# Two FFN layers around a mixer: where the norms' transposes stand, and how far the second token half trails

## The chip, the cores and the metric

The kernel runs on one core of a Trainium2 chip. The metric is device microseconds of one execution, as the median of several runs. Shorter is better.

## What is computed

One decoder layer over 256 tokens of width 2048, in float32. `layer_norm` has scale and shift. The middle line stands for a mixer of differential attention and an RWKV-7 scan with one input projection of 6432 columns; only its output projection matters here.

```python
x = layer_norm(alpha * x + 0.5 * swiglu(x, ffn1_w_gate, ffn1_w_up, ffn1_w_down), ln1_g, ln1_b)
mix = concat([diff_attention(x @ w_in), rwkv7(x @ w_in)]) @ w_out
x = layer_norm(alpha * x + mix, ln2_g, ln2_b)
x = layer_norm(alpha * x + 0.5 * swiglu(x, ffn2_w_gate, ffn2_w_up, ffn2_w_down), ln3_g, ln3_b)

def swiglu(x, w_gate, w_up, w_down):
    return (silu(x @ w_gate) * (x @ w_up)) @ w_down
```

## The kernel before, in words

**Weights and tokens.** The 256 tokens are two halves of 128. Weights come from memory in *pairs*: two blocks of 128 rows by 512 columns, 512 KB, into one of three `raw` buffers (L121, on SyncE's queue). ScalarE rounds a pair to a high part `wh` (L131), VectorE takes the difference as a low part `wl` (L132), and one pair costs each token half six matmuls in `product`: high by high (L139), high by low (L140), low by high (L141). `wh` and `wl` stand in numbered slots, seven in the FFNs and five in the mixer (`NW`). A slot is written anew only when both halves' matmuls with its old pair are done. A `raw` buffer is free when its L132 is done, and only then does the next load into it start.

**Lag.** `block` runs a pair for the first half at once and keeps the second half's turn in a list `pend`, which holds up to `lag` pairs: four in the FFNs, two in the mixer (`LAG`). The first half's sum so ends some pairs before the second half's.

**The FFN's block product.** `two_blocks` does two column blocks for both halves. Of the first eight row blocks it makes seven products in place of eight, of sums and differences of weights and of tokens. Six accumulator banks of PSUM have roles, `a, z, u, w, v, s` in `self.roles`, which change places from one call to the next. The remaining row blocks are done as ordinary pairs (`later`, `late`). At the end of an FFN six such pairs are left for the last block; `flush(lag)` runs them with the second half `lag` pairs behind (L459). At that time the first half's sum is in the bank of role `u` and the second half's in that of `v`.

**The norm.** When a half's last sum is there, `down_done` adds it to the residual (L449; in the mixer `o_done`, L1064), takes statistics (L450 or L1066), and `ln_tail` does the rest on VectorE: L305, L307, a power on GpSimd (L309, 1.0 us), then for each of four column blocks the scaling in two steps (L313, L314). For the norms 1 and 2 each block is then transposed on TensorE in four matmuls by the identity (L76), and split on ScalarE (`xh`, L82) and VectorE (`xl`, L83) as the left operand of the next stage. For norm 3 the blocks go to the output.

**Banks of the transposes.** `tr_bank` gives a bank for each transpose. In the FFNs `ffn_bank` takes, for two of three norm blocks, a bank that it counts from `stream.rot` and from its own count, and a bank `tr` for the third. `rot` isn't changed by `two_blocks`, so which role stands in the bank that is taken isn't looked at.

**The output projection.** The rows of `w_out` come in three parts: the first attention half and the first scan half, then the second attention half, then the second scan half (L1066 belongs to the third part). The third part needs the end of the scan: L863, L869, the head norm (L884, L885, L888, L894 to L899), L902, L904, the gate (L915, L918, L919) and the split of its result (L82, L83). It has four column blocks of two pairs.

**Order.** The program is written in one order, and a scheduler puts each engine's instructions in a row after its own estimate of their times. Each engine then runs its row strictly as it stands.

Of the kernel before, what the change touches and what calls it, by code (L numbers as in the profile page):

```python
# [30 lines left out]
LAG = {"ffn": 4, "mix": 2}  # L31
NW = {"ffn": 7, "mix": 5}
# [7 lines left out]
def build(tc, A, out):  # L40
# [15 lines left out]
    def nm(s):  # L56
        uid[0] += 1
        return f"{s}_{uid[0]}"
# [241 lines left out]
    stream = Stream()  # L300
# [20 lines left out]
    def load_gb(pool, g, b, tg, tb):  # L321
        gt = hp.tile([P, D], F32, tag=tg, name=nm("lng"))
        bt = pool.tile([P, D], F32, tag=tb, name=nm("lnb"))
        nc.gpsimd.dma_start(out=gt, in_=g.to_broadcast([P, D]))
        nc.gpsimd.dma_start(out=bt, in_=b.to_broadcast([P, D]))
        return [[t[:, q * NB:(q + 1) * NB] for q in range(4)] for t in (gt, bt)]

    def load_gb_over_x(g, b):
        gb = [[], []]
        for q in range(4):  # L330
            for i, (t, a) in enumerate((("xh", g), ("xl", b))):
                o = xp.tile([P, NB], F32, tag=f"{t}1{q}", name=nm("lngb"))
                nc.gpsimd.dma_start(out=o, in_=a[:, q * NB:(q + 1) * NB].to_broadcast([P, NB]))
                gb[i].append(o)
        return gb

    def ffn(fp, wg, wu, wd, lg, lb, res, last, extra=None):
# [47 lines left out]
        for half, nj in enumerate((6, 5)):  # L385
# [70 lines left out]
                stream.two_blocks(((wd, n * NB), (wd, (n + 1) * NB)), ks, h_lhs, comb, lambda i, tt, acc, n=n, f=down_done: f(tt, acc, n + i))  # L456
            if half == 1:
                gb.extend(load_gb_over_x(lg, lb))
                stream.flush(LAG["ffn"])  # L459
            j0 += nj  # L460


# [52 lines left out]
    def mix(mp, pq, C):  # L515
# [521 lines left out]
        def ready(q):  # L1037
            stream.drain(gens((a1, a2, r1, r2)[q]))
            for tt in range(2):
                split(res[q][:, :, tt * P:(tt + 1) * P], oT, tt, q)  # L1040
# [16 lines left out]
        def o_done(tt, acc, n, i):  # L1057
            c = slice(n * NB, (n + 1) * NB)
            if i == 0:
                rc = mp.tile([P, NB], F32, tag="tm", name=nm("rc"), bufs=2)  # L1060
                nc.scalar.dma_start(out=rc, in_=xs[tt][:, c])
                V.scalar_tensor_tensor(out=y[tt][n], in0=rc, scalar=ALPHA, in1=acc, op0=ALU.mult, op1=ALU.add)
            else:
                V.tensor_tensor(out=y[tt][n], in0=y[tt][n], in1=acc, op=ALU.add)  # L1064
            if i == len(parts) - 1:
                V.bn_stats(out=st[tt][:, n, :], in_=y[tt][n])  # L1066
                if n == 3:
                    ln_tail(tt, y[tt], st[tt], gb[0], gb[1], False)

        for i, qs in enumerate(parts):  # L1070
            for q in qs:
                ready(q)
            if i == 0:
                yt = [hp.tile([P, 4, NB], F32, tag="J0", name=nm("y")), mp.tile([P, 4, NB], F32, tag="BKc", name=nm("y"))]
                y = [[yt[n // 2][:, 2 * (n % 2) + t, :] for n in range(4)] for t in range(2)]
            if 3 in qs:
                gb.extend(load_gb(mp, A["ln2_g"], A["ln2_b"], "J1", "Q"))
            ks = [(4 * q + j, 4 * q + j) for q in qs for j in range(4)]
            for n in range(4):
                stream.block(A["w_out"][0], n * NB, NB, ks, o_lhs, lambda tt, acc, n=n, i=i: o_done(tt, acc, n, i))  # L1080


    def ffn_bank(pool):
        n = [0]

        def bank(spare=False):
            n[0] += 1
            if spare and n[0] % 3:
                i = (stream.rot + n[0] % 3) % NACC["ffn"]
                return (pa if i < 3 else pool).tile([P, 4, P], F32, tag=f"acc{i}", name=nm("tr"))  # L1090
            return pool.tile([P, 4, P], F32, tag="tr", name=nm("tr"), bufs=2)

        return bank

    with tc.tile_pool(name="fp1", bufs=1) as fp, tc.tile_pool(name="pt1", bufs=1, space=bass.MemoryType.PSUM) as pt:
        tr_bank.append(ffn_bank(pt))
        stream.phase("ffn", fp, pt)
        xc = [fp.tile([P, D], F32, tag=f"y{tt}", name=nm("xc")) for tt in range(2)]

        def load_x(tt, q):  # L1100
            c = slice(q * NB, (q + 1) * NB)
            nc.sync.dma_start(out=xc[tt][:, c], in_=A["x"][0, tt * P:(tt + 1) * P, c])
            transpose_split(xc[tt][:, c], tt, q, xT, tt == 0 and q < 2)

        for q in range(4):
            stream.hooks[2 * q] = [lambda q=q, t=t: load_x(t, q) for t in range(2)]
        xr = [A["x"][0, t * P:(t + 1) * P, :] for t in range(2)]
        C = {}
        ffn(fp, A["ffn1_w_gate"][0], A["ffn1_w_up"][0], A["ffn1_w_down"][0], A["ln1_g"], A["ln1_b"], xr, False,
            lambda after: C.update(mixer_consts(fp, after)))  # L1110
        stream.flush()
    with tc.tile_pool(name="mp", bufs=1) as mp, tc.tile_pool(name="pq", bufs=1, space=bass.MemoryType.PSUM) as pq:
        stream.phase("mix", mp)
        mix(mp, pq, C)
        stream.flush()
# [43 lines left out]
```

## Time and profile before

| what | value |
|---|---|
| three runs, median (lowest to highest) | 1932.76 us (1930.21 to 1933.17) |
| the profiled execution, its own time | 1929.26 us |
| span of that execution, first to last instruction | 1927.5 us |
| TensorE busy | 1888.2 us, 98% of the span |
| VectorE, ScalarE, GpSimd busy | 84%, 57%, 4% |
| bytes moved | 381.73 MB, 198 GB/s in the mean |
| TensorE busy from 20 to 700 us | 679.5 of 680 us |
| TensorE busy from 700 to 720 us (norm 1) | 12.1 of 20 us |
| TensorE busy from 1130 to 1212 us (end of the mixer) | 76.3 of 82 us |
| TensorE busy from 1212 to 1232 us (norm 2) | 15.2 of 20 us |
| TensorE busy from 1232 to 1915 us | 682.5 of 683 us |
| last 12 us of the span (norm 3) | VectorE and the output's transfers |

Rows of the timeline read: start and length in us, engine, line, operation, output from inputs, shapes, and a count where equal rows stand together; in brackets the idle time ahead and what ended it. A matmul row's length (0.39 us) is longer than the distance to the next, since matmuls overlap; the distance from start to start is what a matmul costs.

### The profile page before, as it was taken

The numbers are of one execution on the slowest core, as the hardware profiler recorded it, in microseconds if no ns is written. First come the engines' busy times: TensorE is split into PE (matmuls) and PEld (weight loads), VectorE is DVE, ScalarE is ACT, GpSimd is POOL, SyncE is SP. The second block draws the span as 40 slices with busy tenths as digits, with TensorE's granted clock in tenths as the row PEclk, the third lists the DMA queues.
The fourth block names the chain that finished last, engine by engine and source line by source line (L and its number), as shares of the span: only waits on it lengthen the run. The fifth ranks groups of instructions, "written<-read, shape, count | busy, mean of one in ns | idle before, by whom it ended". The sixth has DMA issues, their size and how long they took to land. (4 is left out here: it accounts for less than half of the span.)

```text
span 1927.5 us, 24928 instructions
## 1 busy us (share of the span) xinstructions
PE 1888.2 (98%) x9335; PEld 1551.1 (80%) x9335; DVE 1620.0 (84%) x1827; ACT 1096.1 (57%) x1372; POOL 71.9 (4%) x108
## 2 busy tenths in 40 slices
PE   9999999999999989999999999899999999999997
PEld 7888888888888878878778877788888888888886
DVE  8999987789999865776677877999999778999995
ACT  5656664466665535645565454566666545666651
POOL 0000101100000000000000000000000110000000
PEclk9999999999999989999999999999999999999999
DMA  9766666666667456555444644775566676666744
GB/s 311 245 202 214 190 237 224 227 205 212 221 210 225 137 159 189 163 164 165 135 136 135 185 148 149 253 261 186 197 207 232 212 246 216 197 204 213 229 151 132
DMA packets 207321, 381.73 MB, mean 198 GB/s; under 512 B 23530, under 2 KB 25648, under 8 KB 206944
## 3 DMA queue, kind: packets, MB, share of 16 engines
q1 hardware_dynamic: 182928, 350.53, 54.9%
q0 software_dynamic: 6832, 15.32, 3.1%
q10 hardware_dynamic: 17440, 14.29, 2.6%
q8 instruction: 73, 1.20, 0.3%
q14 instruction: 48, 0.39, 0.1%
HBM read 368.29 MB, written 11.80 MB: 197 GB/s over the span
## 5 line engine op out<-in xcount | busy, mean ns | idle before, releaser
L131 ACT CAST wh<-raw 128x1024 fp32r<-128x1024 f32 (+2 forms) x833 | 852.5, 1047 | 600.2 <-PE acc L141 358.2
L132 DVE TENSOR_TENSOR wl<-raw,wh 128x1024 fp32r<-128x1024 f32 (+2 forms) x833 | 983.1, 1213 | 214.3 <-ACT wh L131 209.8
L140 PE MATMUL acc<-wl,xh 128*128 128x512 f32 (+1 forms) x1552 | 603.7, 390 | 3.3 <-DVE wl L132 3.3
L141 PE MATMUL acc<-wh,xl 128*128 128x512 f32 (+1 forms) x1552 | 602.2, 390 | 0.0
L139 PE MATMUL acc<-wh,xh 128*128 128x512 f32 (+1 forms) x1552 | 598.1, 392 | 1.1 <-ACT xh L82 0.7
L139 PEld LDWEIGHTS acc<-wh,xh 128*128 128x128 f32 x1552 | 291.8, 188 | 63.3 <-issue 3.0
L140 PEld LDWEIGHTS acc<-wl,xh 128*128 128x128 f32 x1552 | 292.0, 188 | 62.9 <-DVE wl L132 4.3
L141 PEld LDWEIGHTS acc<-wh,xl 128*128 128x128 f32 x1552 | 291.7, 188 | 60.6 <-issue 2.0
L210 DVE TENSOR_TENSOR raw<-raw,raw 128x2048 f32<-128x2048 f32 x112 | 255.8, 2284 | 2.2 <-DMA raw<-in_ffn_w_gate_dram 1.4
L140 PE MATMUL acc<-wl,hh 128*128 128x512 f32 x544 | 212.0, 390 | 0.0
L141 PE MATMUL acc<-wh,hh 128*128 128x512 f32 x544 | 211.3, 389 | 0.0
L139 PE MATMUL acc<-wh,hh 128*128 128x512 f32 x544 | 210.9, 390 | 0.0
L139 PE MATMUL acc<-wh,s 128*128 128x512 f32 x448 | 175.0, 391 | 1.0 <-ACT acc L236 1.0
L141 PE MATMUL acc<-wh,s 128*128 128x512 f32 x448 | 174.5, 389 | 0.0
L140 PE MATMUL acc<-wl,s 128*128 128x512 f32 x448 | 174.4, 389 | 0.0
L139 PEld LDWEIGHTS acc<-wh,hh 128*128 128x128 f32 x544 | 102.1, 188 | 21.7 <-ACT wh L131 0.4
L140 PEld LDWEIGHTS acc<-wl,hh 128*128 128x128 f32 x544 | 102.1, 188 | 21.1
L141 PEld LDWEIGHTS acc<-wh,hh 128*128 128x128 f32 x544 | 102.1, 188 | 21.0
L139 PEld LDWEIGHTS acc<-wh,s 128*128 128x128 f32 x448 | 84.1, 188 | 19.0 <-ACT acc L236 1.4
L141 PEld LDWEIGHTS acc<-wh,s 128*128 128x128 f32 x448 | 84.1, 188 | 17.5
L140 PEld LDWEIGHTS acc<-wl,s 128*128 128x128 f32 x448 | 84.1, 188 | 17.4
L223 ACT COPY acc<-acc 128x512 f32<-128x512 f32 x28 | 16.0, 571 | 50.3 <-PE acc L141 46.2
(261 smaller groups left out, 1103.5 us busy)
## 6 DMA issues: line engine op xcount, KB each, us to landing
raw<-in_ffn_w_up_dram SPq DMA_DIRECT2D x176, 512.0 KB, 5.4
raw<-in_ffn_w_down_dram SPq DMA_DIRECT2D x176, 512.0 KB, 5.6
raw<-in_ffn_w_gate_dram SPq DMA_DIRECT2D x175, 512.0 KB, 4.6
raw<-in_w_in_dram SPq DMA_DIRECT2D x96, 512.0 KB, 3.6
raw<-in_w_out_dram SPq DMA_DIRECT2D x32, 512.0 KB, 3.7
sd<-s POOLq DMA_DIRECT2D x16, 256.0 KB, 3.3
s<-sd POOLq DMA_DIRECT2D x16, 256.0 KB, 5.2
xs<-y ACTq DMA_DIRECT2D x16, 256.0 KB, 3.8
```

The lines of the kernel that those rows point to most:

```text
L131: SC.copy(out=wh[:, c, :w], in_=raw[:, c, :w])
L132: self.cut = V.tensor_tensor(out=wl[:, c, :w], in0=raw[:, c, :w], in1=wh[:, c, :w].bitcast(F32), op=ALU.subtract).ins
L139: T.matmul(a, hi, wh[:, j, :w], start=first and j == 0, stop=False, skip_group_check=True)
L140: T.matmul(a, hi, wl[:, j, :w], start=False, stop=False, skip_group_check=True)
L141: i = T.matmul(a, lo, wh[:, j, :w], start=False, stop=last and j == 1, skip_group_check=True)
L210: V.tensor_tensor(out=out, in0=x, in1=y, op=ALU.subtract)
L223: SC.copy(out=u, in_=a)
```

## The change

Three edits. The flush at an FFN's end lets the second half trail by `NW["ffn"] - 1`, that is six pairs, in place of four; six pairs are all that are left there. Ahead of the third part of the output projection `stream.buffers` sets five slots, as before, and a lag of four in place of two. And when roles are set, the norm's transposes that don't go to `tr` take in turn the banks of the roles 5, 1, 0 and 3, which are `s, z, a, w`.

```diff
@@ ffn
-                stream.flush(LAG["ffn"])
+                stream.flush(NW["ffn"] - 1)
@@ mix, ahead of the third part
             if 3 in qs:
+                stream.buffers(NW["mix"], NW["mix"] - 1)
                 gb.extend(load_gb(mp, A["ln2_g"], A["ln2_b"], "J1", "Q"))
@@ ffn_bank
-        n = [0]
+        n = [0, 0]
         def bank(spare=False):
             n[0] += 1
             if spare and n[0] % 3:
                 i = (stream.rot + n[0] % 3) % NACC["ffn"]
+                if stream.roles is not None:
+                    free = [stream.roles[k] for k in (5, 1, 0, 3)]
+                    n[1] += 1
+                    i = free[n[1] % 4]
                 return (pa if i < 3 else pool).tile([P, 4, P], F32, tag=f"acc{i}", name=nm("tr"))
```

The scheduler answers with other rows at three places. The first is TensorE's row at norm 1, from the second half's last matmul on. `y_2123` is the first half's norm output and `y_2124` the second's; `acc_5828` is the mixer's first column block for the first half, `acc_5847` for the second. Before:

```order
L141 MATMUL acc_5395<-wh_5657,hh_4981 128x512
L76 MATMUL tr_5689<-ident,y_2123 128x128 x4
L76 MATMUL tr_5701<-ident,y_2123 128x128 x4
L76 MATMUL tr_5677<-ident,y_2123 128x128 x4
L76 MATMUL tr_5713<-ident,y_2123 128x128 x4
L76 MATMUL tr_5763<-ident,y_2124 128x128 x4
L76 MATMUL tr_5775<-ident,y_2124 128x128 x4
L139 MATMUL acc_5847<-wh_5824,xh_5768 128x288
```

And now:

```order
L141 MATMUL acc_5395<-wh_5651,hh_4981 128x512
L76 MATMUL tr_5671<-ident,y_2123 128x128 x4
L76 MATMUL tr_5683<-ident,y_2123 128x128 x4
L76 MATMUL tr_5695<-ident,y_2123 128x128 x4
L76 MATMUL tr_5707<-ident,y_2123 128x128 x4
L139 MATMUL acc_5828<-wh_5824,xh_5676 128x288
...
L141 MATMUL acc_5828<-wh_5886,xl_5701 128x288
L76 MATMUL tr_5763<-ident,y_2124 128x128 x4
```

The first half's blocks 0 to 3 (`tr_5677` is block 0 before, `tr_5671` now) are now transposed in their own order, and 30 matmuls of the first half, five pairs of 288 columns, stand ahead of the second half's transposes; before, no matmul did.

The second place is VectorE's row at the end of the scan, where the third part's left operand is made (`xl_10221`, first half). Before:

```order
L899 TENSOR_TENSOR BK_6652<-BK_6652 128x16x64
L132 TENSOR_TENSOR wl_10203<-raw_10200,wh_10202 128x1024
L1064 TENSOR_TENSOR y_9509<-y_9509,acc_10146 128x512
L902 TENSOR_SCALAR BK_6652<-BK_6652,vB 128x4x64 x4
L1064 TENSOR_TENSOR y_9508<-y_9508,acc_10153 128x512
L132 TENSOR_TENSOR wl_10235<-raw_10232,wh_10234 128x1024
L904 TENSOR_TENSOR BK_6652<-BK_6652,vv_6653 128x16x64
L919 TENSOR_TENSOR og_9340<-BK_6652,sm_9341 128x512
L919 TENSOR_TENSOR og_9340<-BK_6652,sm_9366 128x512
L1064 TENSOR_TENSOR y_9509<-y_9509,acc_10186 128x512
L132 TENSOR_TENSOR wl_10255<-raw_10252,wh_10254 128x1024
L83 TENSOR_TENSOR xl_10221<-og_9340,xh_10220 128x512
```

And now, directly behind the same L899:

```order
L132 TENSOR_TENSOR wl_10248<-raw_10245,wh_10247 128x1024
L902 TENSOR_SCALAR BK_6652<-BK_6652,vB 128x4x64 x4
L1064 TENSOR_TENSOR y_9509<-y_9509,acc_10186 128x512
L1064 TENSOR_TENSOR y_9509<-y_9509,acc_10193 128x512
L132 TENSOR_TENSOR wl_10262<-raw_10259,wh_10261 128x1024
L904 TENSOR_TENSOR BK_6652<-BK_6652,vv_6653 128x16x64
L919 TENSOR_TENSOR og_9340<-BK_6652,sm_9341 128x512
L919 TENSOR_TENSOR og_9340<-BK_6652,sm_9366 128x512
L132 TENSOR_TENSOR wl_10282<-raw_10279,wh_10281 128x1024
L1064 TENSOR_TENSOR y_9509<-y_9509,acc_10272 128x512
L132 TENSOR_TENSOR wl_10303<-raw_10300,wh_10302 128x1024
L83 TENSOR_TENSOR xl_10221<-og_9340,xh_10220 128x512
```

Four weight splits (L132) now stand between L899 and that L83, where three stood. On TensorE the scan's own steps have moved back among the projection's matmuls: from the end of L894 to the first matmul that reads `xl_10221` there are now 34 matmuls of 512 columns and L915 and L918; before there were 56 and the same L915 and L918. The last scan step (L863, L869) stands behind 20 of the projection's matmuls; before it stood ahead of all of them. On VectorE, a little earlier, the scan's L851 stands behind the attention's L1010, which waits for a power on GpSimd (L1006), and L832 behind the second such L1010 and an L1018; before, L851 stood ahead of the first L1010 and L832 ahead of the second.

The third place is TensorE's row at the end of the third part. `acc_10363` before and `acc_10348` now are the first half's last column block. Before:

```order
L141 MATMUL acc_10363<-wh_10379,xl_10221 128x512
L139 MATMUL acc_10453<-wh_10359,xh_10224 128x512
...
L141 MATMUL acc_10453<-wh_10379,xl_10225 128x512
L139 MATMUL acc_10370<-wh_10317,xh_10224 128x512
...
L141 MATMUL acc_10370<-wh_10337,xl_10225 128x512
L76 MATMUL at_10399<-ident,y_9508 128x128 x4
```

And now:

```order
L141 MATMUL acc_10313<-wh_10247,xl_10225 128x512
L139 MATMUL acc_10306<-wh_10322,xh_10220 128x512
L139 MATMUL acc_10348<-wh_10344,xh_10220 128x512
L140 MATMUL acc_10306<-wl_10323,xh_10220 128x512
...
L139 MATMUL acc_10348<-wh_10364,xh_10220 128x512
...
L141 MATMUL acc_10348<-wh_10364,xl_10221 128x512
L139 MATMUL acc_10453<-wh_10344,xh_10224 128x512
...
L141 MATMUL acc_10453<-wh_10364,xl_10225 128x512
L76 MATMUL at_10384<-ident,y_9508 128x128 x4
```

Behind the first half's last matmul stood 24 matmuls of the second half, in two column blocks; now there are 12, in one. `wh_10322`, `wh_10344` and `wh_10364` are written to the slots of the third part's first three pairs, `wh_10234`, `wh_10247` and `wh_10261`; the second half uses `wh_10247` for the last time in the first row shown.

## The prediction

> **What bounds the kernel now.** The page first: its first line, and the row of the weights' rounding, the commonest work on ScalarE.
>
> ```profile
> span 1927.5 us, 24928 instructions
> ...
> L131 ACT CAST wh<-raw 128x1024 fp32r<-128x1024 f32 (+2 forms) x833 | 852.5, 1047 | 600.2 <-PE acc L141 358.2
> ```
>
> ScalarE's idle time is mostly put down to TensorE's L141: it waits for slots. TensorE itself is busy through both FFNs, so only the three norms and the mixer's end hold time that a new order can move. Norm 1 next, TensorE's timeline:
>
> ```profile
> 688.80 0.39 PE L141 MATMUL acc<-wh,hh 128*128 128x512 f32 x1
> ...
> 702.40 0.39 PE L141 MATMUL acc<-wh,hh 128*128 128x512 f32 x1
> 702.72 0.63 PE L76 MATMUL tr<-ident,y 128*128 128x128 f32 x4
> ...
> 705.90 0.66 PE L76 MATMUL tr<-ident,y 128*128 128x128 f32 x4 [1.27 <-DVE y L449]
> 710.00 1.12 PE L76 MATMUL tr<-ident,y 128*128 128x128 f32 x4 [3.45 <-DVE xl L83]
> 713.67 1.97 PE L76 MATMUL tr<-ident,y 128*128 128x128 f32 x8 [2.55 <-DVE y L314]
> ...
> 717.36 0.38 PE L141 MATMUL acc<-wh,xl 128*128 128x288 f32 x1
> 717.57 0.29 PE L139 MATMUL acc<-wh,xh 128*128 128x288 f32 x1
> 717.70 0.29 PE L140 MATMUL acc<-wl,xh 128*128 128x288 f32 x1
> ```
>
> The first two rows are 60 matmuls apart: 0.227 us for 512 columns, so 1.36 us for a pair of one half. A matmul of 288 columns costs 0.13 us (717.57 to 717.70). The FFN's last sum is done at 702.40, and the mixer's matmuls run from about 717.4. The third transpose waits for L449: the first half's block 0 goes into the bank of the second half's sum. Idle in these rows: 1.27 + 3.45 + 2.55 = 7.3 us.
>
> **Norm 1: the banks and the longer flush.** VectorE's and ScalarE's rows there:
>
> ```profile
> 696.03 0.69 DVE L449 TENSOR_TENSOR y<-y,acc 128x512 f32<-128x512 f32 x1 [2.97 <-PE acc L141]
> ...
> 705.17 0.68 DVE L449 TENSOR_TENSOR y<-y,acc 128x512 f32<-128x512 f32 x1
> ...
> 712.87 1.41 DVE L314 SCALAR_TENSOR_TENSOR y<-y,rs,lngb 128x512 f32<-128x512 f32 x2
> ```
>
> ```profile
> 707.89 0.67 ACT L131 CAST wh<-raw 128x576 fp32r<-128x576 f32 x1 [1.69 <-DMA raw<-in_w_in_dram]
> ```
>
> The first half's sum ended 30 matmuls ahead of 702.40, at 695.60; L449 followed 0.43 us later, and I take that as the way from one engine to the next. The second half now trails by 36 matmuls: 1.36 us earlier. So the second half's L449 moves from 705.17 to 703.8. Its last steps gain less, since a split of the weights that are cast at 707.89 stands in front of them: L314 comes at about 711.95, 0.9 us earlier. On TensorE the four transposes follow 702.40 at 0.63 us each, to 705.2. Then come 30 matmuls, 30 x 0.13 = 3.9 us, the last of them after the split of the late weights (707.89 + 0.67, and as much again on VectorE: 709.3), to 710. The second half's transposes start 0.9 us earlier, and the 3.9 us of matmuls are behind TensorE by then: 4.8 us gained. The loads that follow come no more than about 4 us earlier, so I take back 0.3 (0 to 1). The term is **-4.5 us**; bounds are -3.4 (the second half's chain is no earlier, and part of the loads is late) and -6 (the late weights come sooner). The transposes do wait for nothing but their inputs now; the next thing that is late is the second half's chain on VectorE. In the flush the first half takes its sixth pair 1.36 us sooner; it now needs that pair at 693.1 (695.60 less five matmuls, less 1.36). The pair's split is ahead of the 2.97 us for which VectorE idles until 696.03, so it is done by 693.06 at the latest: it costs nothing; uncovered it would be up to 1.4 us.
>
> **The scan's last steps.** VectorE, GpSimd and TensorE ahead of the projection:
>
> ```profile
> 1154.72 0.42 DVE L851 TENSOR_TENSOR St<-sm,St 128x256 f32<-128x256 f32 x1 [0.69 <-PE sm L846]
> ```
>
> ```profile
> 1155.30 1.01 POOL L1006 TENSOR_TENSOR ars<-vr,neghalf 128x4 f32<-128x4 f32 x1 [32.66 <-DVE vr L1004]
> ```
>
> ```profile
> 1160.63 0.68 PE L869 MATMUL sm<-AR,St 64*64 64x64 f32 x16
> 1161.32 0.50 PE L139 MATMUL acc<-wh,xh 128*128 128x512 f32 x1
> ```
>
> L851 now waits in VectorE's row for a GpSimd power of 1.0 us that starts, after its own input, at about 1154.3: L851 comes at 1155.9. L832 stands behind the second such power and so comes at about 1160.1. The attention's steps come sooner in exchange, and the projection's first matmul at about 1162.0, 0.65 us later than 1161.32; L863 and L869, 16 small matmuls each and 0.6 us by the row at 1160.63, 1.25 us together, are then still to do. **+1.9 us**, between 0 (the power is quicker than VectorE needs it) and 3.
>
> **The third part's start.** TensorE at L894 and behind L918, then VectorE:
>
> ```profile
> 1172.77 1.89 PE L894 MATMUL sm<-BK,bones 128*128 128x256 f32 x8
> ...
> 1182.95 0.50 PE L140 MATMUL acc<-wl,xh 128*128 128x512 f32 x1
> ```
>
> ```profile
> 1178.85 1.23 DVE L899 TENSOR_TENSOR BK<-BK 128x1024 f32<-128x1024 f32 x1 [4.93 <-ACT BK L897]
> 1179.99 1.22 DVE L132 TENSOR_TENSOR wl<-raw,wh 128x1024 fp32r<-128x1024 f32 x1
> 1181.13 0.68 DVE L1064 TENSOR_TENSOR y<-y,acc 128x512 f32<-128x512 f32 x1
> 1181.72 1.38 DVE L902 TENSOR_SCALAR BK<-BK,vB 128x256 f32<-128x256 f32 x4
> 1183.02 0.68 DVE L1064 TENSOR_TENSOR y<-y,acc 128x512 f32<-128x512 f32 x1
> 1183.61 1.22 DVE L132 TENSOR_TENSOR wl<-raw,wh 128x1024 fp32r<-128x1024 f32 x1
> 1184.75 1.22 DVE L904 TENSOR_TENSOR BK<-BK,vv 128x1024 f32<-128x1024 f32 x1
> 1186.07 1.28 DVE L919 TENSOR_TENSOR og<-BK,sm 128x512 f32<-128x512 f32 x2
> ...
> 1189.00 1.29 DVE L83 TENSOR_TENSOR xl<-og,xh 128x512 fp32r<-128x512 f32 x2
> ```
>
> TensorE: 10.18 us from L894 to the row at 1182.95, with 19 projection matmuls (4.3) in it, so 5.9 for L894, L915 and L918. Before, 56 projection matmuls stood between L894 and the first use of `xl_10221`: 5.9 + 12.7 = 18.6 us after L894's start, and the first L83 was done 16.9 after it (1189.65). The operand came 1.7 us early. Now 34 stand there: 5.9 + 7.7 = 13.6. And VectorE needs from L899, 6.08 after L894, start to start: L899 1.14, four L132 4.56, L902 1.30, three L1064 1.77, L904 1.32, two L919 1.2, L83 0.7: it is done 18.1 after L894. TensorE waits 18.1 - 13.6, **+4.5 us**, with the whole projection queued behind. With VectorE as quick as before it would be 16.9 - 13.6 = 3.3; with one more rounding and split in the way (1.05 + 1.2), 6.7. That is the largest term; I find nothing that hides it.
>
> **Five slots under a lag of four.** The order shows the waits: `wh_10344` can be rounded only when `wh_10247` has had its last matmul, and TensorE reaches it two matmuls behind that. 0.43 + 1.05 (L131's mean) + 0.05 - 2 x 0.227 = 1.1 us. `wh_10364` needs rounding and split, 0.43 + 1.05 + 1.23, against eight matmuls (1.8): 0.9. **+2.0 us**, between 1 and 3 (a load that is late too).
>
> **Norm 2.** The last sum, the first transpose, the first half's last L1064, and the loads of the next weights:
>
> ```profile
> 1212.57 0.39 PE L141 MATMUL acc<-wh,xl 128*128 128x512 f32 x1
> 1216.54 1.12 PE L76 MATMUL at<-ident,y 128*128 128x128 f32 x4 [3.58 <-DVE y L314]
> ```
>
> ```profile
> 1207.56 0.69 DVE L1064 TENSOR_TENSOR y<-y,acc 128x512 f32<-128x512 f32 x1
> ...
> 1208.84 1.23 DVE L132 TENSOR_TENSOR wl<-raw,wh 128x1024 fp32r<-128x1024 f32 x1 [0.60 <-ACT wh L131]
> ```
>
> ```profile
> raw<-in_ffn_w_gate_dram SPq DMA_DIRECT2D x175, 512.0 KB, 4.6
> ```
>
> The first transpose stood 9.4 us behind the first half's last matmul (1212.57 less 24 matmuls is 1207.13), of which 5.44 were covered by the second half. Now 12 matmuls cover 2.72. The chain itself gets longer: the split ahead of its L305 takes weights whose buffer the last pair's split frees, about 0.9 us ahead of the first half's end; with 3.6 to 4.6 for the load, 1.05 and 1.2 it ends 4.9 to 5.9 behind that end. At 1208.84 it ended 2.9 behind. One L1066 less stands there. 10.4 to 11.3 in place of 9.4; less the cover, 7.7 to 8.6 idle in place of 4.0. What follows runs behind the same chain. **+3.7 us**, between 1.5 (the load is there in time) and 5.
>
> **Norm 3.** VectorE's rows:
>
> ```profile
> 1908.76 0.69 DVE L449 TENSOR_TENSOR y<-y,acc 128x512 f32<-128x512 f32 x1 [2.15 <-PE acc L141]
> ...
> 1915.88 0.68 DVE L449 TENSOR_TENSOR y<-y,acc 128x512 f32<-128x512 f32 x1
> ```
>
> The second half's sum could be taken at 1908.76 + 30 x 0.227 = 1915.56; VectorE is busy with the first half until 1915.88. Moved 1.36 us ahead, the first half is out of the way: **-0.3 us** (0 to -0.4). The rest of the tail, 12 us on VectorE and the output's transfers, stays.
>
> **The sum.** -4.5 + 1.9 + 4.5 + 2.0 + 3.7 - 0.3 = +7.3 us on the profiled execution: 1929.26 (its span of 1927.5 and 1.8 around it) becomes 1936.6. The median of the runs is 3.5 above that execution; 1932.76 + 7.3 = 1940.1. No difference under 0.2%, 3.9 us, can be told from no change.
>
> **TensorE's clock, and a rule.** Two windows and a row:
>
> ```profile
> 997.38 0.50 PE L140 MATMUL acc<-wl,xh 128*128 128x512 f32 x1 [2.18 <-DVE wl L132]
> ```
>
> ```profile
> 997.00:1000.00 3.00, 2.62 (x12) 1.00 0.51 146
> ...
> 1217.00:1220.00 3.00, 2.29 (x10) 0.50 0.98 269
> ```
>
> After a wait of 2.18 us the granted clock stayed 1.00; after the 3.58 at norm 2 it was 0.50 for 3 us. The new wait at the third part comes in two pieces of about 2.7 and 1.8 us with four matmuls between, which lies between these rows; I take none of it. The Trainium skill, "TensorE: Matmul & The Clock Gate", section "Why this matters for your kernels", says to leave no TensorE gap of more than about 3 us, or the clock falls to half: by that rule each piece, being shorter, leaves the clock alone; were the two taken for one gap, it would fall. That is the first rival.
>
> **The rivals.** *The clock falls at the third part as well.* For it: norm 2's row; against it: 997.38. 3 us at 0.50 do 1.5 us of work, and I estimate 2 with the way back to full speed: 1942.1. *VectorE keeps up.* The scan's end costs nothing (0 for the scan's steps, and for the third part only 0.5, since the split weights wait and the chain goes first), the other terms as above: -4.5 + 0 + 0.5 + 2.0 + 3.7 - 0.3 = +1.4, 1934.2, no change. For it: in the trace of before no wait stands there. Against: the order within an engine is fixed, and four L132 stand in front. *Faster: the mixer's end is quick throughout.* One mechanism: rounding follows TensorE so closely that neither operand nor slot is waited for. Then norm 1 decides alone: -4.5 - 0.3 and 1.5 for norm 2, -3.3; with the upper gain of 6, -4.8: 1928.0. It decides if the waits at the third part and the slots come to less than 1 us together; the row at 997.38 shows a wait of the same kind, for L132, that did cost 2.18. *The change does not do what it says* holds in part in the forecast already: the second half trails by two pairs, not by four, at the projection's end.
>
> **How the numbers follow.** Forecast 0.53, clock 0.15, VectorE keeps up 0.21, faster 0.11. Slower by over 0.2% (above 1936.6) are the first two, 0.68; within it the third, 0.21; faster (below 1928.9) the last, 0.11. With every low bound the sum is -6 + 0 + 3.3 + 1 + 1.5 - 0.4 = -0.6, with every high one -3.4 + 3 + 6.7 + 3 + 5 = +14.3; not all fall to one side, so the range ends at +12.5 above and reaches to -1.5 below, which takes in the third case and leaves the faster one out: 1931.3 to 1945.3.
>
> **What would show it right or wrong.** In the new profile the third transpose of norm 1 waits for L314 and not for L449, and 30 matmuls stand ahead of the second half's transposes (right for -4.5). The first use of `xl_10221` waits for L83 for 1 us or more, and its high part before it (right for +4.5; with no such wait the forecast falls to the third case). Two waits of about 1 us for L131 and L132 stand in the third part. The first transpose of norm 2 stands 7 to 9 us behind the last sum; at 4 or less the term is wrong. Total TensorE waits between 1150 and 1232 that are no longer than before would make the prediction wrong as a whole.

## The result

The change makes the kernel slower: 1941.52 us in the median of five runs (1940.29 to 1944.18) against 1932.76 us (1930.21 to 1933.39). The ratio is 1.0051, with a 95% interval of 1.0036 to 1.0065; on 1932 us that is 9.9 us (7.0 to 12.6). The two medians lie 8.8 us apart. Here and below, what a kernel is slower or faster by is taken from the ratio, on 1932 us; for the experiments it departs from the plain difference of medians by up to 1 us.

### The profile after

The profiled execution took 1944.18 us, the longest of the five. The page's first line:

```profile
span 1942.4 us, 24926 instructions
```

**Norm 1** on TensorE's timeline (start, length, engine, line, shapes, count; in brackets the idle time ahead and what ended it):

```profile
702.18 1.91 PE L76 MATMUL tr<-ident,y 128*128 128x128 f32 x16
704.17 0.37 PE L139 MATMUL acc<-wh,xh 128*128 128x288 f32 x1
...
708.75 0.40 PE L140 MATMUL acc<-wl,xh 128*128 128x288 f32 x1 [0.40 <-DVE ve L307]
712.21 1.94 PE L76 MATMUL tr<-ident,y 128*128 128x128 f32 x8 [2.54 <-DVE y L314]
```

The first half's sixteen transposes run in one piece. The wait of 1.27 us for the second half's sum (L449) is gone, and 30 matmuls of the mixer stand ahead of the second half's transposes. The wait that is left, for L314, is as long as before (2.55 there).

**The scan's end**, the same view, and then windows of it (busy us of each engine with counts, and the granted clock, the third number from the end):

```profile
1156.03 0.44 PE L1017 MATMUL at<-ident,ot 128*128 128x128 f32 x2 [0.73 <-DVE ot L1013]
1159.33 0.66 PE L1017 MATMUL at<-ident,ot 128*128 128x128 f32 x2 [1.85 <-DVE ot L1013]
1161.22 0.79 PE L139 MATMUL acc<-wh,xh 128*128 128x512 f32 x1 [0.18 <-ACT xh L82]
...
1164.37 0.63 PE L139 MATMUL acc<-wh,xh 128*128 128x512 f32 x1
1164.79 0.63 PE L140 MATMUL acc<-wl,xh 128*128 128x512 f32 x1
```

```profile
1158.00:1160.00 2.00, 0.67 (x4) 0.45 (x6) 1.56 (x6) 0.00 (x0) 0.14 (x1) 0.77 0.00 0
1160.00:1162.00 2.00, 1.82 (x18) 1.54 (x19) 1.29 (x3) 1.14 (x2) 0.00 (x0) 0.50 0.03 8
1162.00:1164.00 2.00, 2.00 (x7) 1.51 (x6) 0.81 (x2) 0.37 (x1) 0.00 (x0) 0.50 0.00 0
1164.00:1166.00 2.00, 2.00 (x6) 1.58 (x5) 0.00 (x0) 0.00 (x0) 0.00 (x0) 0.52 0.00 0
```

VectorE's rows there:

```profile
1154.41 0.16 DVE L1010 TENSOR_TENSOR ars<-ars,fl 128x4 f32<-128x4 f32 x1 [0.83 <-POOL ars L1006]
1158.17 0.16 DVE L1010 TENSOR_TENSOR ars<-ars,fl 128x4 f32<-128x4 f32 x1 [0.76 <-POOL ars L1006]
...
1159.36 0.41 DVE L832 COPY Rs<-sm 128x256 f32<-128x256 f32 x1
```

TensorE waits twice for the attention's L1013, which stands behind L1010 and so behind GpSimd's power. Behind the waits the clock is 0.50: matmuls of 512 columns start 0.42 us apart (1164.37 to 1164.79), where they take 0.227 at full clock. Before, the clock stayed at 1.00 here.

**The third part and norm 2**, the same view, with two windows:

```profile
1192.70 0.50 PE L139 MATMUL acc<-wh,xh 128*128 128x512 f32 x1 [0.94 <-DVE y L1064]
1197.38 0.50 PE L139 MATMUL acc<-wh,xh 128*128 128x512 f32 x1 [1.66 <-ACT xh L82]
1199.83 0.63 PE L141 MATMUL acc<-wh,xl 128*128 128x512 f32 x1 [1.25 <-DVE xl L83]
...
1211.54 0.50 PE L139 MATMUL acc<-wh,xh 128*128 128x512 f32 x1 [0.90 <-ACT wh L131]
1220.86 0.50 PE L140 MATMUL acc<-wl,xh 128*128 128x512 f32 x1 [0.77 <-DVE wl L132]
...
1221.89 0.39 PE L141 MATMUL acc<-wh,xl 128*128 128x512 f32 x1
1223.78 0.67 PE L139 MATMUL acc<-wh,xh 128*128 128x512 f32 x1 [1.50 <-DVE y L1064]
...
1227.99 0.40 PE L141 MATMUL acc<-wh,xl 128*128 128x512 f32 x1
1232.97 1.12 PE L76 MATMUL at<-ident,y 128*128 128x128 f32 x4 [4.58 <-DVE y L314]
```

```profile
1199.00:1202.00 3.00, 2.17 (x6) 1.70 (x7) 1.37 (x3) 0.00 (x0) 0.00 (x0) 0.68 0.84 273
1202.00:1205.00 3.00, 3.00 (x12) 2.42 (x11) 0.96 (x2) 0.00 (x0) 0.00 (x0) 0.76 0.14 51
```

None of these waits stood in the rows before norm 2 of the first kernel. The first, 0.94, is for an accumulator bank, of which the mixer has three: L1064, which empties it, comes late in VectorE's row. Two are for the late left operand (1.66 for `xh`, 1.25 for `xl`), and two come from the slots (L131, L132). The one at 1223.78 is for a bank again: the second half's last block starts only when L1064 has emptied one.

### Thirteen profiles, four stretches

The experiments below gave eleven more profiles. To compare stretches and not sums, I take five marks that every trace has: the last matmul of the first FFN; the mixer's L140 that waits 2.2 us for L132 (at 997.38 in the first profile); the start of L894 at the scan's end; the projection's last matmul; and a row of the second FFN that waits about 0.5 us for L236 (1821.13 in the first profile). In us:

| kernel | first mark to second: norm 1, part of the mixer | second to L894 | L894 to the projection's end | projection's end to last mark: norm 2, most of FFN 2 |
|---|---|---|---|---|
| before | 294.98 | 175.39 | 39.80 | 608.56 |
| before, again (e10) | 296.21 | 176.85 | 39.80 | 608.55 |
| full change | 292.05 | 182.27* | 51.72* | 608.47 |
| full change, again (e11) | 292.11 | 181.44* | 48.98* | 610.47 |
| banks (e1) | 293.28 | 176.79 | 39.80 | 609.51 |
| flush (e2) | 294.75 | 181.43* | 43.86* | 608.56 |
| lag of four (e3) | 297.17 | 177.18 | 45.25 | 610.74 |
| banks and flush (e4) | 291.37 | 182.19* | 43.83* | 608.84 |
| the same, pinned (e5) | 291.73 | 178.24 | 39.80 | 608.83 |
| full change, pinned (e6) | 291.21 | 178.23 | 45.28 | 610.07 |
| banks, last flush (e7) | 293.54 | 176.75 | 39.81 | 608.57 |
| lag of three (e8) | 296.33 | 176.83 | 39.80 | 608.96 |
| waits filled (e9) | 291.29 | 179.70* | 41.73* | 609.42 |

A star: 24 of the projection's matmuls (19 in e9) stand ahead of L894 here that stood behind it; 24 x 0.227 = 5.45 us (4.31) is taken from the second stretch and put on the third, so that equal work is compared.

### The profile page after: what moved, and what is told of

It reads as the page before. It is cut to its first block, busy times and chain, and to the rows that moved or that the text cites. A ratio compares the mean times of both kernels' runs of the same rounds, so it can differ in the third digit from the quotient of the medians.

```text
span 1942.4 us, 24926 instructions
## 1 busy us (share of the span) xinstructions
PE 1897.6 (98%) x9335; PEld 1555.6 (80%) x9335; DVE 1620.2 (83%) x1827; ACT 1094.7 (56%) x1372; POOL 72.5 (4%) x108
## 5 line engine op out<-in xcount | busy, mean ns | idle before, releaser
L131 ACT CAST wh<-raw 128x1024 fp32r<-128x1024 f32 (+2 forms) x833 | 851.5, 1047 | 612.4 <-PE acc L141 374.0
L132 DVE TENSOR_TENSOR wl<-raw,wh 128x1024 fp32r<-128x1024 f32 (+2 forms) x833 | 982.5, 1213 | 225.3 <-ACT wh L131 220.7
L140 PE MATMUL acc<-wl,xh 128*128 128x512 f32 (+1 forms) x1552 | 607.0, 392 | 5.4 <-DVE wl L132 5.0
L141 PE MATMUL acc<-wh,xl 128*128 128x512 f32 (+1 forms) x1552 | 605.1, 391 | 2.0 <-DVE xl L83 2.0
L140 PEld LDWEIGHTS acc<-wl,xh 128*128 128x128 f32 x1552 | 293.8, 189 | 66.3 <-DVE wl L132 7.3
L141 PEld LDWEIGHTS acc<-wh,xl 128*128 128x128 f32 x1552 | 292.9, 189 | 64.4 <-DVE xl L83 3.3
L140 PE MATMUL acc<-wl,hh 128*128 128x512 f32 x544 | 212.0, 390 | 0.0
L141 PE MATMUL acc<-wh,hh 128*128 128x512 f32 x544 | 211.4, 389 | 0.0
L141 PE MATMUL acc<-wh,s 128*128 128x512 f32 x448 | 174.5, 389 | 0.0
L140 PE MATMUL acc<-wl,s 128*128 128x512 f32 x448 | 174.4, 389 | 0.0
L141 PEld LDWEIGHTS acc<-wh,hh 128*128 128x128 f32 x544 | 102.1, 188 | 21.1
L140 PEld LDWEIGHTS acc<-wl,hh 128*128 128x128 f32 x544 | 102.1, 188 | 21.1
L140 PEld LDWEIGHTS acc<-wl,s 128*128 128x128 f32 x448 | 84.1, 188 | 17.5 <-DVE wl L132 0.2
L141 PEld LDWEIGHTS acc<-wh,s 128*128 128x128 f32 x448 | 84.1, 188 | 17.5
```

Of the source, the lines that this page charges most:

```text
L131: SC.copy(out=wh[:, c, :w], in_=raw[:, c, :w])
L132: self.cut = V.tensor_tensor(out=wl[:, c, :w], in0=raw[:, c, :w], in1=wh[:, c, :w].bitcast(F32), op=ALU.subtract).ins
L140: T.matmul(a, hi, wl[:, j, :w], start=False, stop=False, skip_group_check=True)
L141: i = T.matmul(a, lo, wh[:, j, :w], start=False, stop=last and j == 1, skip_group_check=True)
```

## The experiments

My theory was that each term of the sum hangs on rows that the scheduler moved. The rival was that the loss is the third part's longer lag, and all else a small gain. The order of the program already split them: with the flush edit alone, the scan's end has nearly the rows of the full change (36 matmuls behind L894 in place of 34), though that edit is 450 us ahead of them; with the lag alone, it has the rows of before.

### e1 to e4: the edits apart

e1 has the bank edit alone.

> Only the bank edit; both flushes and the lag of the third part as before. Theory by terms (mine): the scan's end and the third part keep the rows of before, so nothing is lost there, and norm 1 gives what the banks give without the second half's earlier chain, 3.4 us: 1929.4 us. The first half's four transposes stand directly behind the second half's last FFN matmul with no wait, and the mixer's matmuls of the first half ahead of the second half's transposes. Rival (the banks are worth little, since the second half's chain on VectorE sets the end of norm 1 anyway): -1 us or less, 1932.

Measured: 1929.83 us, ratio 0.9987 (0.9978 to 0.9996), 2.5 us faster. TensorE's rows at norm 1:

```profile
704.52 0.66 PE L76 MATMUL tr<-ident,y 128*128 128x128 f32 x4 [0.68 <-DVE y L314]
709.42 0.40 PE L140 MATMUL acc<-wl,xh 128*128 128x288 f32 x1 [0.39 <-DVE wl L132]
713.78 2.79 PE L76 MATMUL tr<-ident,y 128*128 128x128 f32 x12 [3.43 <-DVE y L314]
```

The first half's fourth block follows L314, not L449, with a wait of 0.68 where I had expected none; the second half's chain is no earlier than before, so its wait is 3.43. The first stretch is 2.9 us shorter than the mean of the two of before with e3 and e8, which have the same rows there (296.17). That fits my theory; the time by itself, with its interval of 0.8 to 4.3 us, doesn't rule out the rival, but the stretch does.

e2 has the flush edit alone:

```diff
-                stream.flush(LAG["ffn"])
+                stream.flush(NW["ffn"] - 1)
```

> Only the flush edit; banks and the third part's lag as before. Its order moves the scan's last steps behind the attention's L1010 and leaves 36 matmuls of 512 columns between L894 and the first use of the third part's left operand (56 before), exactly as in the full change, although the lag of the third part is two. Theory by terms: -1 at norm 1, -0.3 at norm 3, +1.9 at the scan's end, 18.1 - (5.9 + 36 x 0.227) = +4.0 at the third part, together +4.6, 1937.4 us; +2 more (1939) if the clock falls as it did in the full change at 1160 to 1166. Rival (the loss belongs to the third part's longer lag alone): -1 to -2 us, 1931 us, with no wait of TensorE over 1 us at the scan's end.

Measured: 1939.20 us, ratio 1.0038 (1.0025 to 1.0051), 7.3 us slower. TensorE's rows, from the scan's end and the third part:

```profile
1158.87 0.44 PE L1017 MATMUL at<-ident,ot 128*128 128x128 f32 x2 [0.73 <-DVE ot L1013]
1162.17 0.66 PE L1017 MATMUL at<-ident,ot 128*128 128x128 f32 x2 [1.85 <-DVE ot L1013]
...
1199.63 0.50 PE L139 MATMUL acc<-wh,xh 128*128 128x512 f32 x1 [1.83 <-ACT xh L82]
1201.85 0.49 PE L140 MATMUL acc<-wl,xh 128*128 128x512 f32 x1 [0.64 <-DVE wl L132]
```

The two waits for L1013 are those of the full change to the hundredth. The rival is out: the flush edit, at the first FFN's end, loses at the scan's end. The third stretch grew by 4.1 (4.0 expected for 36 matmuls), the second by 4.6. The time is the 1939 that the theory gave for a fall of the clock, and the clock did fall, from 1161.4 to 1168.3 us.

e3 has the lag of four alone:

```diff
             if 3 in qs:
+                stream.buffers(NW["mix"], NW["mix"] - 1)
```

> Only the lag of four in the third part; banks and flush as before. The scan's end keeps the rows of before; 45 matmuls of 512 columns stand between L894 and the first use of the third part's left operand. Theory by terms: 16.9 - (5.9 + 45 x 0.227) = +0.8 at the third part, +2.0 for the slots, +1.5 for an accumulator bank ahead of the second half's last block, +3.7 at norm 2: +6.5 to +8, 1939.3 to 1940.8 us. Rival (the whole loss of the change is the lag's): the full loss and the gain of norm 1 together, +12 to +13, 1945 us. Third (a longer trail is harmless by itself, the loss is the scan's end): 0 to +2, at most 1935 us.

Measured: 1938.13 us, ratio 1.0036 (1.0024 to 1.0049), 7.0 us slower. The loss is within the theory's 6.5 to 8; the time itself is 1.2 us under the lowest that it gave. TensorE's waits from L894 on:

```profile
1193.65 0.50 PE L139 MATMUL acc<-wh,xh 128*128 128x512 f32 x1 [0.69 <-ACT wh L131]
1207.24 0.50 PE L139 MATMUL acc<-wh,xh 128*128 128x512 f32 x1 [0.81 <-ACT wh L131]
1216.51 0.50 PE L140 MATMUL acc<-wl,xh 128*128 128x512 f32 x1 [0.76 <-DVE wl L132]
1219.43 0.50 PE L139 MATMUL acc<-wh,xh 128*128 128x512 f32 x1 [1.48 <-DVE y L1064]
1229.32 1.11 PE L76 MATMUL at<-ident,y 128*128 128x128 f32 x4 [6.89 <-DVE y L314]
```

No wait for the left operand, with 45 matmuls ahead of it; the theory had 0.8 us there. The slots and the bank cost 5.45 us in the third stretch, norm 2 about 2 in the fourth. The brackets come to 3.74 only: the start at 1193.65 is 1.08 behind the matmul ahead of it, 0.85 more than a matmul costs, and the next follows after 0.33, 0.11 more than usual, 0.96 lost in all. Counted so, the four waits lose 0.96, 1.18, 1.09 and 1.76: a wait on TensorE here costs its bracket and about 0.3. That makes 5.0; the other 0.5 us of the stretch I can't place.

e4 has banks and flush, without the lag.

> Bank and flush edits together, the third part's lag two as before. Theory by terms: norm 1 and norm 3 give the full -4.8, the scan's end and the third part take +1.9 and +4.0: +1.1, 1933.9 us; 1935.9 if the clock falls at the scan's end. Rival (the loss belongs to the lag): -4.8, 1928 us. If the edits add up, e1 + e2 - before is the same within 1.5 us.

Measured: 1935.04 us, ratio 1.0017 (1.0009 to 1.0026), 3.3 us slower. With the lag the edits add up: 3.3 for these two and 7.0 are 10.3, and the full change loses 9.9. Banks and flush by themselves add up less well: -2.5 + 7.3 = 4.8, not 3.3. That is 1.5 us apart, by the plain medians 1.9, where I had allowed 1.5; the intervals are too wide to tell it from chance.

### e5 and e6: the scan's order pinned

If the flush loses only through the order at the scan's end, then it should gain once that order is held. In e5 (banks and flush) and e6 (the full change) the first of the two last L1010 is issued only behind the scan's L851, the second behind L832. That changes VectorE's order and nothing that is computed.

```diff
-                        V.tensor_tensor(out=Sn, in0=ps, in1=St, op=ALU.add)
+                        st["seen"] = V.tensor_tensor(out=Sn, in0=ps, in1=St, op=ALU.add).ins
...
-                V.tensor_copy(out=Rs, in_=ps)
+                rs_copy = V.tensor_copy(out=Rs, in_=ps).ins
+                if c == 3:
+                    st["seen2"] = rs_copy
...
-                V.tensor_tensor(out=rs, in0=rs, in1=fl, op=ALU.mult)
+                pin = r2.get("seen" if h == 2 else "seen2") if g == 1 and h >= 2 else None
+                with tc.issue_after(pin) if pin is not None else ExitStack():
+                    V.tensor_tensor(out=rs, in0=rs, in1=fl, op=ALU.mult)
```

> Banks and flush as in the change, the third part's lag two as before, and VectorE's row at the scan's end pinned: the first of the two last L1010 is issued only behind the scan's L851, the second behind L832, as in the order of before; again 56 matmuls stand between L894 and the first use of the third part's left operand. The computation is the same. Theory (the flush edit loses only through the rows that the scheduler moved at the scan's end): its waits of 0.7 and 1.9 us for L1013, the half clock behind them and the 1.8 us for xh are gone, and norm 1 and norm 3 are left: -2.3 (bank edit alone, measured) -1.1 (norm 1 with the flush edit, by the two traces) -0.4 (norm 3) = -3.8, 1928.3 us. Rival (the flush costs in itself, or the clock falls elsewhere): it stays near banks and flush without the pin, 1935 us, +3.

Measured: 1927.59 us, ratio 0.9976 (0.9966 to 0.9985), 4.6 us faster. The rows that answer to those at 1156.03 and 1159.33 (lines are shifted by four):

```profile
1154.39 0.44 PE L1021 MATMUL at<-ident,ot 128*128 128x128 f32 x2 [0.44 <-DVE ot L1017]
1155.95 0.66 PE L1021 MATMUL at<-ident,ot 128*128 128x128 f32 x2 [0.32 <-DVE ot L1017]
```

The waits are 0.44 and 0.32, the third stretch is 39.80 as before, and the second only 1.4 longer than usual. The 7.9 us between e4 and e5 are the price of the moved rows.

The half clock at this place is not gone, though, as the theory had said. In this profile it fell from 1155.89 to 1162.73 us, with no wait over 0.44 us near it:

```profile
1158.00:1160.00 2.00, 2.00 (x19) 1.69 (x20) 1.12 (x2) 0.68 (x2) 1.14 (x2) 0.50 0.22 41
```

So the long waits for L1013 are not needed for a fall here.

> The full change with the same pin; 45 matmuls stand between L894 and the first use of the third part's left operand, 12 behind the first half's last. Theory (losses add up: the order at the scan's end and the lag of four each on its own): the +6.0 of the lag alone on top of -3.8, +2.2, 1934.3 us. Rival A (the lag only hurt because the scan's end was late): below 1930 us. Rival B (the pin does nothing with the long lag): 1941.5 us.

Measured: 1934.62 us, ratio 1.0011 (1.0002 to 1.0020), 2.1 us slower than before. The losses add up (-4.6 + 7.0 = +2.4); both rivals are out. Its profile has the same waits at the scan's end as e5, and there the clock stayed at 1.00 from 1156 to 1166 us.

### e7: the longer flush at the second FFN's end only

```diff
-                stream.flush(LAG["ffn"])
+                stream.flush(NW["ffn"] - 1 if last else LAG["ffn"])
```

> Bank edit, and the flush edit for the second FFN only, so that nothing ahead of the second FFN's end is changed against the bank edit alone. Theory: norm 3 gives 0.3 to 0.4 more than the bank edit alone, 1929.4 us. Rival (the flush costs slots in itself): slower than the bank edit alone by 1 us or more, 1931 us.

Measured: 1928.13 us, ratio 0.9980 (0.9970 to 0.9990), 3.9 us faster. From the last mark to the end of the execution e1 takes 1929.16 - 1821.00 = 108.16 us and e7 1929.40 - 1821.58 = 107.82: 0.34 less, the term of norm 3. The medians differ by more than that, and their intervals overlap.

### e8: a lag of three

```diff
             if 3 in qs:
+                stream.buffers(NW["mix"], 3)
```

> Kernel before with a lag of three, not two and not four, in the third part. The rows at the scan's end are those of before, 56 matmuls ahead of the left operand, 24 behind the first half's last, and one slot is spare: 18 matmuls of the second half stand between a slot's last use and its next one. Theory (the lag of four loses by slots, by the accumulator bank and by the shorter cover of norm 2, none by trailing as such): 0, within 1 us, 1932 us, with no wait of TensorE for L131 or L132 in the third part. Rival (trailing as such costs): +3 us, half of the lag of four.

Measured: 1931.95 us, ratio 1.0001 (0.9992 to 1.0010). The third stretch is 39.80, with no wait for L131 or L132. Trailing as such costs nothing; the fourth pair does, with five slots and three banks. A sixth slot would tell slots and banks apart further; no run has one.

### e9: work in the waits

What share of the scan's end is the clock? e9 is e4 with transposes of the identity, which nobody reads, in the two waits for L1013.

```diff
+                if g == 1 and h >= 2:
+                    idle = bank("pr", (P, 4, P))
+                    with tc.issue_after(r2["a2" if h == 2 else "q3"]):
+                        for i in range(4 if h == 2 else 10):
+                            T.transpose(idle[:, i % 4, :], ident, ident)
                 tr = bank("at", (P, 4, P))
```

> Banks and flush without the pin, and idle work in two waits of the scan's end: 4 transposes of the identity ahead of the first of the two last L1017 and 10 ahead of the second, 0.6 and 1.5 us by the rate of 0.15 us each, into a bank that nobody reads. The scheduler moves rows behind them: 5 fewer projection matmuls stand ahead of L894, 37 in place of 36 between L894 and the third part's left operand, and one L132 in place of four on VectorE's way to it, 14.7 against 14.3 us. Theory (the clock falls because of the two waits, and costs 3 us there): from the wait at 994 to L894 it takes 187.6 - 5 x 0.227 - 3 = 183.5 us, the granted clock stays at 1.00 behind the waits, the third part waits 0.4 in place of 2.8, and the time is 1935.0 - 3 - 3.6 = 1928.4 us. Rival (the clock falls by the scan's small matmuls, or the work behind waits for something else anyway): 186.5 us for that stage and 1931.4 us.

Measured: 1933.36 us, ratio 1.0011 (1.0002 to 1.0020), above both forecasts. TensorE's rows there, and windows as above:

```profile
1157.36 1.31 PE L1019 MATMUL pr<-ident 128*128 128x128 f32 x10
1159.18 0.44 PE L1022 MATMUL at<-ident,ot 128*128 128x128 f32 x2 [0.51 <-DVE ot L1013]
```

```profile
1160.00:1162.00 2.00, 1.49 (x20) 1.21 (x21) 1.53 (x4) 1.51 (x3) 0.00 (x0) 1.00 0.00 0
1162.00:1164.00 2.00, 2.00 (x10) 1.64 (x9) 0.33 (x1) 0.00 (x0) 0.00 (x0) 1.00 0.00 0
```

The clock stayed at 1.00, and the second stretch, 184.01 us as it stands, is near the theory's 183.5 and far from the rival's 186.5. Against e4 it is 2.5 us shorter, and 1.7 to 2.6 against the four profiles of that order. I put that down to the clock, but the rows moved as well, and by e5 and e6 the clock falls or holds in this place with the same rows, so one profile doesn't show it. The sum missed: the third part waited 1.66 us for L1064's bank, which neither theory had, in place of 0.4, and the first FFN took 0.9 longer in this execution. The stretches together gain 4.1 on e4 and the median only 1.7: e4's profiled execution is the slowest of its eleven, 1.45 above their median, and with the 0.9 of the first FFN that is the difference. In four of e9's eleven executions the mean granted clock was 0.991, and these took 1934.70 to 1936.72 us; in the other seven it was 0.993 or 0.994, and they took 1930.92 to 1933.86. So the transposes don't keep the clock up every time, though no trace shows where those four lost it.

### e10 and e11: both kernels once more

> The kernel before, unchanged, for a second profile of it. In the first, the clock stayed at 1.00 behind the 2.18 us wait at 997; the same wait in eight of the nine other profiles was followed by about 3.4 us at 0.50, 1.7 us lost. Norm 1's wait for xl was 3.45 there and 4.61 and 3.32 in two others with the same rows. Theory (the first profile was a quick one by these two): the clock falls this time, and the execution takes 1930.5 to 1932.5 us. Rival (the bank edit or others make the clock fall): it stays at 1.00, 1929.5 us.

Measured: 1932.86 us, 3.6 more than the first profile and 0.4 above the theory's range; the clock fell, and the rival is out. Behind the wait that was followed by a clock of 1.00 in the first profile, one window for each us:

```profile
999.48 0.50 PE L140 MATMUL acc<-wl,xh 128*128 128x512 f32 x1 [2.18 <-DVE wl L132]
```

```profile
999.48:1000.48 1.00, 1.00 (x3) 0.86 (x4) 1.00 (x2) 0.24 (x1) 0.00 (x0) 0.72 0.02 2
1000.48:1001.48 1.00, 1.00 (x4) 0.72 (x4) 1.00 (x3) 0.00 (x0) 0.00 (x0) 0.50 0.85 164
1001.48:1002.48 1.00, 1.00 (x5) 0.80 (x4) 1.00 (x2) 0.00 (x0) 0.00 (x0) 0.50 0.89 344
1002.48:1003.48 1.00, 1.00 (x5) 0.77 (x4) 1.00 (x5) 0.00 (x0) 0.36 (x1) 0.58 0.08 29
1003.48:1004.48 1.00, 1.00 (x6) 0.83 (x5) 0.09 (x2) 0.12 (x1) 0.65 (x1) 1.00 0.85 203
```

The lost share is 0.28 + 0.50 + 0.50 + 0.42 = 1.70 us. So the first profile was a quick one: the first FFN 0.87 shorter, norm 1 1.23, and the clock with 1.46, together the 3.6.

> The full change, unchanged, for a second profile of it. The first profiled execution took 1944.18 us, the median of five is 1941.52. Theory (what differs between its executions is how often the clock falls and how long the first weights take, while the waits stay): every wait of TensorE at the scan's end and in the third part is there again within 0.1 us, the clock falls behind the waits of 0.7 and 1.9 us and behind those at 1197 and 1200 or in one of the two places only, 1.7 to 3 us a place, and the execution takes 1940 to 1943 us. Rival (the waits themselves were longer in the first profile): the third part's waits come to 2 us less, with the clock as before.

Measured: 1945.39 us, above the range I gave; the first FFN took 2.75 us longer. The waits at the scan's end are there again (0.73, 1.85), with the clock at half behind them. TensorE's rows in the third part and at norm 2:

```profile
1194.67 0.63 PE L139 MATMUL acc<-wh,xh 128*128 128x512 f32 x1 [0.94 <-DVE y L1064]
...
1197.65 0.63 PE L140 MATMUL acc<-wl,xh 128*128 128x512 f32 x1
...
1200.93 0.50 PE L139 MATMUL acc<-wh,xh 128*128 128x512 f32 x1 [1.66 <-ACT xh L82]
...
1202.27 0.50 PE L141 MATMUL acc<-wh,xl 128*128 128x512 f32 x1
...
1234.23 1.12 PE L76 MATMUL at<-ident,y 128*128 128x128 f32 x4 [6.61 <-DVE y L314]
```

The same waits begin, but the clock fell in other places: already behind the wait of 0.94, where matmuls of 0.63 us stand, and not behind the operand. The 1.25 us for `xl` are no longer shown ahead of 1202.27, but the wait for `xh` is as long as it was. ScalarE's rows say why:

```profile
1199.31 1.04 ACT L131 CAST wh<-raw 128x1024 fp32r<-128x1024 f32 x1 [0.80 <-PE acc L141]
1200.27 1.14 ACT L82 CAST xh<-og 128x512 fp32r<-128x512 f32 x2
```

`xh` (L82) stands behind a rounding (L131) that waits until TensorE's L141 has freed a slot, so the slow matmuls put `xh` back as well. The first use of `xl` stands 18.57 us behind L894 (1183.70 to 1202.27) where it stood 18.11: of the 1.7 us that the fall takes, 0.5 show. Ahead of norm 2 the clock did not fall, and the wait there is 6.61 in place of 4.58: the third stretch gave back 2.7 us and the fourth took 2.0 of it. So the waits are not all the same within 0.1 us, as my theory had it; where the clock falls decides whether a fall adds to a wait or fills it.

## Why the prediction was right, and where it was not

The direction and the size were right: 1940.1 forecast, 1941.52 measured, in the range. Its base and some of its terms were off, and that the number fits so well is in part luck: between the marks of the profiles the change costs 13.7 us, not 7.3 (below), while the medians lie only 8.8 apart.

**Norm 1 (-4.5): right.** The first stretch takes 292.05 and 292.11 us against a mean of 296.17: -4.1. The third transpose waits for nothing, where the sign that I gave was a wait for L314; the 30 matmuls stand where the order had them, and the wait left is for L314. From e1, about 2.9 of it are the banks'.

**The scan's last steps (+1.9): the waits right, the size not.** TensorE's idle brackets from 1150 to the projection's first matmul come to 3.62 us (0.19, 0.34, 0.33, 0.73, 1.85, 0.18) against 1.75 before (0.19, 0.44, 0.77, 0.35): +1.9, as worked out. But the stretch grew by 5.4 (4.6 in the second profile) against e10, where the clock fell behind the 2.2 us wait as it did in the change. The rest is half clock: from 1159.09 to 1165.93 us it takes 3.4 us of work. The failed step is the one that counted the waits of this place and left the clock at full speed. What made it fall is open: it fell in all four profiles with the two long waits, but also in e5 without them, and not in e6. e9 puts 1.7 to 2.6 us on the clock, with the reservation made there.

**The third part's start (+4.5): right.** The first use of `xl` stands 18.11 us behind L894 (1181.72 to 1199.83); 18.1 was worked out from VectorE's rows. The brackets are 0.94 + 1.66 + 1.25 = 3.85, or 4.7 with 0.3 for each. The waits follow the count of matmuls ahead: with 34 they come to 3.85, with 36 to 2.8 (0.35, 1.83 and 0.64 in e2), with 45 and 56 to nothing. e9, with 37, has the operand in time and waits 1.66 for a bank. Half clock came on top: in the two windows from 1199 it loses 3 x 0.32 + 3 x 0.24 = 1.7 us, all of it behind the waits, in dense matmuls.

**Five slots (+2.0): right.** 0.90 and 0.77 where 1.1 and 0.9 stood, 2.3 with 0.3 for each.

**Norm 2 (+3.7): the chain right, the mark not.** The first transpose stands 11.08 us behind the first half's last matmul (1221.89 to 1232.97); 10.4 to 11.3 was the forecast. In the second profile it is 11.5 (1222.69 to 1234.23). But it stands 4.98 us behind the last sum, not 7 to 9: the twelve matmuls behind it took 6.1 us, not 2.72, with a wait of 1.5 for a bank and the clock at half. The chain hid those losses: in the second profile, with the clock at full speed there, 7.00 us stand behind the last sum (1227.23 to 1234.23). The bank was missed altogether.

**Norm 3 (-0.3): right**, -0.4 from the last mark to the end (1944.18 - 1836.46 = 107.72 against 108.13).

**The rivals.** That VectorE keeps up and that the mixer's end is quick are out: the waits are there. The clock's fall was a missing piece, beside the bank. Its time, 1942.1, is nearer than the forecast's. In both profiles the clock fell in the third part, as it had said, and at the scan's end as well, which it had not named.

**The clock, as I read it, was the wrong inference.** I took the row at 997.38, 2.18 us idle and then 1.00, for what such a wait does. The same wait stands in all thirteen profiles, 2.17 or 2.18 us long; in eleven of them (all but the first of before and e5) the clock fell, up to 1.5 us later, and 1.7 us were lost. The Trainium skill, "TensorE: Matmul & The Clock Gate", section "Why this matters for your kernels", advises no gaps of more than about 3 us; by these runs 2.2 us is already too long, most times. Its section "What's actually happening" speaks of a free-running window of 3.4 us: the 1.70 us lost at half clock, that is 3.4 us, agree with its length, and that the same wait is not always followed by a fall agrees with a window that the program does not set. Shorter waits were mostly harmless: of nine waits of 1.48 to 1.90 us in the third part, in seven profiles, two had a fall within 3 us, both in the first profile of the change.

**The base.** The sum was made against an execution that e10 shows to be quick by 2.7 us between the marks; the shift to the median took that in. From the first mark to the last the two profiles of the change take 1134.5 and 1133.0 us, those of before 1118.7 and 1121.4: 13.7 in the mean, where the runs as a whole differ by 9.9 (8.8 by the medians). Both profiled executions of the change are longer than the other four; what those did better isn't shown by any trace, and stays open. It is hardly the clock alone: over the longest execution, e11, the mean granted clock was 0.991, over the other four 0.989 to 0.990.

**Which edit.** The prediction priced places, not edits. The runs name them: banks -2.5, flush +7.3 (about -2 by its own place, which is e5 less e1, and 8 from the scan's order that it shifts, which is e4 less e5; that leaves 1.5 unplaced), lag +7.0. The change without the lag and with the scan's order held has the lowest ratio of all versions run, 0.9976 (0.9966 to 0.9985); e7, at 0.9980 (0.9970 to 0.9990), can't be told from it.

## What to carry to other kernels

Where a scheduler writes the order, an edit's price lies wherever rows moved, not where the code was edited: compare the whole order for each edit alone, and pin what must not move. A trail behind the first half was free here while a slot and a bank were to spare (a lag of three), and cost 7 us with the pair that used up the last one. Price a wait on TensorE as its bracket and 0.3 us around it. Keep a price for half clock beside it, 1.7 us, likely at 2.2 us of wait (11 of 13 profiles) and possible at any length seen here, and take two profiles before trusting a row that says otherwise.

## What the hardware did that I had not expected

Behind a wait of 0.94 us the clock fell in one profile of two (1194.67 in e11, not 1192.70 in the first), while waits of 1.83 and 1.90 us in the third part of e2 and e4 had no fall behind them. With fourteen transposes into an unread bank it stayed at full speed through the two waits at the scan's end in the one profile taken, where the four profiles of that order without them show nearly 7 us at half. The length of a wait by itself does not tell whether the clock falls. The first FFN, whose rows were the same up to its last block, ended between 701.62 and 704.70 us in the thirteen profiles, a spread as large as most terms here.
